# The squared-ReLU MLP of a conformer layer: all first products, then all second products, with the squares kept in DRAM between them

## The chip, the cores and the metric

The kernel runs on one core of a Trainium2 chip. A core has five engines that run their own instruction queues in order: PE (TensorE, matrix products, with a separate row PEld for its weight loads), DVE (VectorE), ACT (ScalarE), POOL (GpSimd) and SP (SyncE, which here only issues DMAs). The metric is the device time of one execution in microseconds (us).

## The reference

One layer on 512 tokens of width 2048: a conformer convolution block, then the MLP, then a last norm. The change touches only the MLP.

```python
h = rmsnorm(x, norm1_g[0]);  x = x + conformer_conv(h, ...)
x = x + sq_relu_mlp(rmsnorm(x, norm2_g[0]), mlp_w1[0], mlp_w2[0])
return rmsnorm(x, final_g)

def sq_relu_mlp(h, w1, w2):
    return jnp.square(jax.nn.relu(h @ w1)) @ w2     # w1: 2048 x 8192, w2: 8192 x 2048
```

## The kernel before

All values are float32, and every product is made of three matmuls of a high part (the value rounded to the matmul type `fp32r`, made by a cast on ACT) and a low part (value minus high part, made by a subtraction): `mm3` at L265 to L270. So each weight chunk that PE uses needs, ahead of it, a DMA, a cast and a subtraction.

**First product.** The width 8192 is cut into 64 tiles f of 128 columns. A tile takes 2 chunks of w1 (128x1024 each) and 48 matmuls of 512 columns. A chunk's low part is made by DVE or POOL (`Plain`, L113). The result is scaled and clipped (L792, DVE) and squared (L793, ACT).

**Second product.** It is made by a seven-product scheme (Winograd's form of Strassen's). Two neighbouring tiles f make a pair; its squares are four 128x256 blocks ("four"), from which three further block sums ("sums") are formed, and the seven blocks are split into high (`ah`) and low (`al`) parts, 128x1792 each (L797, L798). Four pairs make a group; there are 8 groups. On the weight side a group has two halves q, and a half has 14 factors: seven products P1 to P7, each for the inner halves 0 and 1. I write P5.1 for product P5 of inner half 1, and `Factor.make` (L138) builds it: three of the seven are a loaded block as it is (P1, P2, P3), and four are a difference, written in place over a block by POOL (P5 L149, P6 L152, P7 L155, P4 L158). So P5's subtraction may start only once P1's low part has been made from the same block, P6's only after P5's, and so on. Then comes the cast (ACT, L159), two copies of the high part into PSUM (ACT, L162, the tile `ax`) and two subtractions on DVE that read one input from PSUM (L163). A factor takes PE 12 matmuls. The order of the factors in a half is P1.0, P5.0, P2.0, P1.1, P5.1, P2.1, P6.0, P6.1, P3.0, P3.1, P7.0, P7.1, P4.0, P4.1; of P1.1, P5.1 and P2.1 the first six matmuls of each come first, then the other six of each. Finished sums are added from PSUM into the residual on DVE (L834).

**The order before.** Group by group: 8 tiles of the first product, their blocks, then both halves of the second product of the group. The last group has only four tiles in the seven-product form; its other four tiles go through a plain second product with 16 chunks of `w2b`.

**What sets the order of the instructions.** The program is written in the order of the mathematics, and a list scheduler, with its own model of the times, fixes for each engine an order that the engine then follows strictly. A chunk or factor is prepared four ahead of its use (`Stream.AHEAD`), in four buffers `wh` and `wl`: the cast of a factor has to wait until PE is done with the factor four before it.

Of the kernel before, what the change touches and what calls it, by code (L numbers as in the profile page):

```python
# [12 lines left out]
F32 = mybir.dt.float32  # L13
# [5 lines left out]
P = 128  # L19
T = 512  # L20
# [9 lines left out]
POOL_TAPS = 6  # L30

# [29 lines left out]
LEFT = {"P1": 0, "P7": 1, "P4": 2, "P2": 3, "P5": 4, "P6": 5, "P3": 6}  # L61
# [4 lines left out]
OPENS = ("P1", "P5", "P2")  # L66

# [8 lines left out]
def trunk(ctx: ExitStack, tc: tile.TileContext, xT, vec, fg, w_in, w_out, w1, w2s, w2b, out):  # L76
# [10 lines left out]
    front = ExitStack()  # L87
    early = front.enter_context(tc.tile_pool(name="early", bufs=1))
# [41 lines left out]
    class Factor:  # L130
# [7 lines left out]
        def make(self, hi, lo):  # L138
# [20 lines left out]
            nc.scalar.copy(out=hi, in_=s)  # L159
            for sl in (slice(0, 512), slice(512, 1024)):  # L160
                st = bank("ax")
                nc.scalar.copy(out=st, in_=hi[:, sl].bitcast(F32))  # L162
                nc.vector.tensor_tensor(out=lo[:, sl], in0=s[:, sl], in1=st, op=sub)  # L163
# [26 lines left out]
    for q in range(4):  # L190
        items += [Plain(w_out[q, c], nc.gpsimd) for c in range(0 if q else 4, 8)]
    for g in range(NG):
        items += [Plain(w1[g * GROUP + f, c], nc.gpsimd if c else nc.vector) for f in range(GROUP) for c in range(2)]
        if g < NG - 1:
            for q in range(2):
                sums = Sums(w2s[g, q])
                items += [Factor(sums, *x) for x in ORDER]
        else:
            for q in range(2):
                sums = Sums(w2s[g, q])  # L200
                items += [Factor(sums, x, 0) for x, hs in ORDER if hs == 0]
# [55 lines left out]
    def split_scaled(src, g, name):  # L257

        hi = big.tile([P, T], F32R, tag="hh", name=f"{name}h")
        lo = big.tile([P, T], F32R, tag="hl", name=f"{name}l")  # L260
# [331 lines left out]
    class Norm:  # L592


        def __init__(self, k, halves, lo_eng):
            if len(vs) == k:
                vs.append((big.tile([P, T], F32R, tag="hh", name="vh"), big.tile([P, T], F32R, tag="hl", name="vl")))
# [155 lines left out]

    acc = []
    row2 = None
    for g in range(NG):
        last = g == NG - 1
        a = []
        for f in range(GROUP):
            ps = bank()  # L760
            for c in range(2):
                wh, wl = chunk()
                for i in range(8):
                    k = 8 * c + i
                    sl = slice(i * P, (i + 1) * P)
                    mm3(ps, (wh[:, sl], wl[:, sl]), h2[k], k == 0, k == NT - 1)
            if row2 is None:
                st = bank("ax")
                col_sums(st, acc1)
                ms = tmp.tile([P, NTOK], F32, tag="st", name="ms")  # L770
                nc.vector.tensor_scalar(out=ms, in0=st[:, :NTOK], scalar1=1.0 / D, scalar2=None, op0=ALU.mult)
                r2 = spread(inv_sqrt(ms, eps_rms, RMS_EPS, NTOK))
                row2 = shift
                nc.scalar.copy(out=row2, in_=r2)

                for b in range(NTOK):
                    for n in range(4):
                        x2 = big.tile([P, 512], F32, tag="da", name=f"x2_{b}_{n}")
                        pt = bank("ax")
                        for i in range(4):  # L780
                            nc.tensor.transpose(out=pt[:, i * P : (i + 1) * P], in_=xt[4 * n + i][:, b * P : (b + 1) * P], identity=ident)
                        nc.scalar.copy(out=x2, in_=pt)
                        acc.append(x2)
                front.close()
                mlp[0] = ctx.enter_context(tc.tile_pool(name="mlp", bufs=4, reuse_waits="tile"))
            if f % 2 == 0:
                hi = mlp[0].tile([P, 7 * HT], F32R, tag="ah", name="ah")
                lo = mlp[0].tile([P, 7 * HT], F32R, tag="al", name="al")
                four = mlp[0].tile([P, 4 * HT], F32, tag="rb", name="four", bufs=5)
                a.append((hi, lo))  # L790
            here = four[:, f % 2 * T :][:, :T]
            nc.vector.scalar_tensor_tensor(out=here, in0=ps, scalar=0.0, in1=row2, op0=ALU.max, op1=ALU.mult)  # L792
            nc.scalar.activation(out=here, in_=here, func=AF.Square)  # L793

            def split(x, at):
                sl = slice(at * HT, at * HT + x.shape[-1])
                nc.scalar.copy(out=hi[:, sl], in_=x)  # L797
                nc.vector.tensor_tensor(out=lo[:, sl], in0=x, in1=hi[:, sl].bitcast(F32), op=ALU.subtract)  # L798

            a21, a11, a22, a12 = (four[:, i * HT : (i + 1) * HT] for i in range(4))  # L800
            if last and f >= GROUP // 2:
                split(here, f % 2 * 2)
            elif f % 2 == 0:
                sums = mlp[0].tile([P, 4 * HT], F32, tag="rb", name="sums", bufs=5)
# [4 lines left out]
            else:  # L809
# [3 lines left out]
                nc.vector.tensor_tensor(out=s4, in0=a12, in1=s2, op=ALU.subtract)  # L813
                split(sums[:, HT:], 4)

        def seven(q):

            banks = {}

# [134 lines left out]
```

## Time and profile before

| | us |
|---|---|
| median of 3 runs | 1949.85 (1948.09 to 1950.24) |
| the profiled execution: its time | 1946.68 |
| the profiled execution: its span | 1944.8 |
| PE busy | 1889.1 (97%) |
| DVE, ACT, POOL busy | 1251.7, 970.3, 911.2 |

The span is the time from the first to the last instruction. The first product of the MLP begins at 580.71 us. In a row of the timeline stand the start, the duration, the engine, the line, the operation, what it writes and reads, the shape, and in brackets how long the engine had been idle and what released it. Back-to-back matmuls overlap, so a matmul of 0.39 us starts every 0.227 us. In the table by stretches each engine has its busy time, and PEclk is the granted share of TensorE's clock.

### The profile page before, as it was taken

The numbers are of one execution on the slowest core, as the hardware profiler recorded it, in microseconds if no ns is written. First come the engines' busy times: TensorE is split into PE (matmuls) and PEld (weight loads), VectorE is DVE, ScalarE is ACT, GpSimd is POOL, SyncE is SP. The second block draws the span as 40 slices with busy tenths as digits, with TensorE's granted clock in tenths as the row PEclk, the third lists the DMA queues.
The fourth block names the chain that finished last, engine by engine and source line by source line (L and its number), as shares of the span: only waits on it lengthen the run. The fifth ranks groups of instructions, "written<-read, shape, count | busy, mean of one in ns | idle before, by whom it ended". The sixth has DMA issues, their size and how long they took to land.

```text
span 1944.8 us, 22992 instructions
## 1 busy us (share of the span) xinstructions
PE 1889.1 (97%) x8578; PEld 1559.8 (80%) x8578; DVE 1251.7 (64%) x1752; ACT 970.3 (50%) x1406; POOL 911.2 (47%) x475
## 2 busy tenths in 40 slices
PE   6999999989999999999999999999999999999998
PEld 4888888888888877877887887787788778778876
DVE  8999999981044566476466557645754764664485
ACT  5444444473245465367337536634743663473362
POOL 5799999756542252244234224423522442442343
PEclk9999999999999999999999999999999999999999
DMA  5222333114222223322322332232233223223333
GB/s 209 90 98 87 104 123 120 44 52 177 98 97 76 98 97 109 130 81 82 109 87 98 119 130 98 72 102 98 76 130 120 98 87 112 72 91 126 119 93 103
DMA packets 59728, 199.99 MB, mean 103 GB/s; under 512 B 6624, under 2 KB 7264, under 8 KB 59616
## 3 DMA queue, kind: packets, MB, share of 16 engines
q1 hardware_dynamic: 59184, 197.41, 30.0%
q8 instruction: 67, 1.10, 0.2%
q10 hardware_dynamic: 432, 1.11, 0.2%
q14 instruction: 45, 0.37, 0.1%
HBM read 194.31 MB, written 4.19 MB: 102 GB/s over the span
## 4 chain that ended last, share of the span: by engine, by line
PE 71%; DVE 9%; issue 8%; POOL 5%; ACT 4%; DMA 3%; SPq 0%; POOLq 0%; DVEq 0%; ACTq 0%
PE mm L269 21%; PE mm L270 20%; PE mm L268 20%; PE mm L639 8%; DMA b<-in_w2s 2%; POOL b L149 2%; ACT wh L159 2%; DVE wl L163 2%; DVE ax L344 1%; ACT ax L162 1%; POOL b L155 1%; POOL b L158 1%; POOL b L152 1%; DVE x L834 1%; DVE sums L813 1%
## 5 line engine op out<-in xcount | busy, mean ns | idle before, releaser
L113 POOL TENSOR_TENSOR wl<-raw,wh 128x1024 fp32r<-128x1024 f32 x151 | 365.1, 2428 | 620.9 <-ACT wh L112 618.3
L112 ACT CAST wh<-raw 128x1024 fp32r<-128x1024 f32 (+1 forms) x221 | 230.1, 1047 | 452.3 <-PE mm L269 252.4
L269 PE MATMUL mm<-yl,wh 128*128 128x512 f32 x1024 | 398.7, 389 | 0.2 <-DVE yl L262 0.2
L268 PE MATMUL mm<-yh,wh 128*128 128x512 f32 x1024 | 398.7, 389 | 0.0
L270 PE MATMUL mm<-yh,wl 128*128 128x512 f32 x1024 | 398.6, 389 | 0.0
L163 DVE TENSOR_TENSOR wl<-b,ax 128x512 fp32r<-128x512 f32 x420 | 270.2, 681 | 132.1 <-ACT ax L162 95.0
L269 PE MATMUL mm<-wl,ah 128*128 128x512 f32 x840 | 330.1, 393 | 20.4 <-DVE wl L163 20.4
L268 PE MATMUL mm<-wh,ah 128*128 128x512 f32 x840 | 327.0, 391 | 2.3 <-DVE x L834 1.5
L270 PE MATMUL mm<-wh,al 128*128 128x512 f32 x840 | 327.0, 389 | 0.0
L159 ACT CAST wh<-b 128x1024 fp32r<-128x1024 f32 x210 | 217.7, 1050 | 161.8 <-POOL b L149 77.9
L162 ACT COPY ax<-wh 128x512 f32<-128x512 f32 x420 | 234.1, 584 | 13.2 <-DVE wl L163 10.5
L269 PEld LDWEIGHTS mm<-yl,wh 128*128 128x128 f32 x1024 | 192.2, 188 | 40.2 <-DVE yl L262 0.6
L270 PEld LDWEIGHTS mm<-yh,wl 128*128 128x128 f32 x1024 | 192.2, 188 | 40.0
L268 PEld LDWEIGHTS mm<-yh,wh 128*128 128x128 f32 x1024 | 192.2, 188 | 39.7
L344 DVE SCALAR_TENSOR_TENSOR ax<-u,v,ax 128x512 f32<-128x512 f32 x327 | 218.0, 749 | 0.0
L268 PE MATMUL mm<-xh,wh 128*128 128x512 f32 (+1 forms) x544 | 206.9, 380 | 5.9 <-ACT wh L112 5.4
L269 PE MATMUL mm<-xl,wh 128*128 128x512 f32 (+1 forms) x544 | 207.4, 381 | 2.5 <-DVE xl L262 2.4
L270 PE MATMUL mm<-xh,wl 128*128 128x512 f32 (+1 forms) x544 | 206.6, 380 | 3.0 <-DVE wl L113 3.0
L269 PEld LDWEIGHTS mm<-wl,ah 128*128 128x128 f32 x840 | 157.6, 188 | 63.8 <-DVE wl L163 32.3
L268 PEld LDWEIGHTS mm<-wh,ah 128*128 128x128 f32 x840 | 157.6, 188 | 38.3 <-DVE x L834 2.5
L270 PEld LDWEIGHTS mm<-wh,al 128*128 128x128 f32 x840 | 157.7, 188 | 32.0
L149 POOL TENSOR_TENSOR b<-b,b 128x1024 f32<-128x1024 f32 x30 | 74.6, 2486 | 213.6 <-DVE wl L163 213.6
(171 smaller groups left out, 2479.8 us busy)
## 6 DMA issues: line engine op xcount, KB each, us to landing
raw<-in_w SPq DMA_DIRECT2D x128, 512.0 KB, 3.3
b<-in_w2s SPq DMA_DIRECT2D x120, 512.0 KB, 3.6
raw<-in_w_in SPq DMA_DIRECT2D x63, 512.0 KB, 3.3
raw<-in_w_out SPq DMA_DIRECT2D x32, 512.0 KB, 3.3
xt<-in_xT SPq DMA_DIRECT2D x16, 256.0 KB, 5.9
xr<-in_xT SPq DMA_DIRECT2D x16, 256.0 KB, 4.6
raw<-in_w2b SPq DMA_DIRECT2D x16, 256.0 KB, 2.8
out<-x SPq DMA_DIRECT2D x15, 256.0 KB, 2.9
```

What stands on the lines that cost most here:

```text
L112: nc.scalar.copy(out=hi[:, sl], in_=raw[:, sl])
L113: (nc.vector if sl.stop == cut else self.eng).tensor_tensor(out=lo[:, sl], in0=raw[:, sl], in1=hi[:, sl].bitcast(F32), op=ALU.subtract)
L149: nc.gpsimd.tensor_tensor(out=s, in0=b12, in1=b11, op=sub)
L152: nc.gpsimd.tensor_tensor(out=s, in0=b22, in1=b11, op=sub)
L159: nc.scalar.copy(out=hi, in_=s)
L162: nc.scalar.copy(out=st, in_=hi[:, sl].bitcast(F32))
L163: nc.vector.tensor_tensor(out=lo[:, sl], in0=s[:, sl], in1=st, op=sub)
L268: nc.tensor.matmul(out=ps, lhsT=wh, rhs=xh, start=first, stop=False, **how)
L269: nc.tensor.matmul(out=ps, lhsT=wh, rhs=xl, start=False, stop=False, **how)
L270: nc.tensor.matmul(out=ps, lhsT=wl, rhs=xh, start=False, stop=last, **how)
L344: nc.vector.scalar_tensor_tensor(out=o, in0=a, scalar=w, in1=c, op0=ALU.mult, op1=ALU.add)
L639: nc.tensor.matmul(out=ps[n][:, sl], lhsT=a[:, wsl], rhs=x[:, sl], start=first and a is wh and x is hi, stop=last and x is lo)
```

## The change

The first product is now made for all 64 tiles in one go. Of each pair the four blocks and the three sums are written to DRAM (`spill`, 128x1792, by two DMAs on ACT's queue), the sums being made by POOL instead of DVE. Then the second product runs through all 8 groups without a first product between them. `fetch` reads a pair back (SP's queue, two buffers `seven`), `prepare` casts it on ACT in two pieces of 768 and 1024 columns and makes the low parts on DVE. Seven slots hold prepared pairs; slots 3 to 6 lie in the memory of the first product's input `h2`. In the second product, P2's low part is made by POOL straight from the block and its cast (`LO_POOL`), with no copies into PSUM and nothing on DVE. Memory pools are opened from two ends of SBUF. The number of matmuls and their operands' sizes do not change.

```diff
+LO_POOL = ("P2",)
+SLOTS = 7
+PREP = ((0, 3), (0, 9), (1, 2), (1, 12))
+FETCH = ((0, 0), (0, 4), (0, 10), (1, 3))
...
             nc.scalar.copy(out=hi, in_=s)
+            if self.product in LO_POOL:
+                nc.gpsimd.tensor_tensor(out=lo, in0=s, in1=hi.bitcast(F32), op=sub)
+                return
             for sl in (slice(0, 512), slice(512, 1024)):
...
+    for f in range(FF // P):
+        items += [Plain(w1[f, c], nc.gpsimd if c else nc.vector) for c in range(2)]
     for g in range(NG):
-        items += [Plain(w1[g * GROUP + f, c], nc.gpsimd if c else nc.vector) for f in range(GROUP) for c in range(2)]
...
+    def fetch(n):
+        raws[n] = mlp[0].tile([P, 7 * HT], F32, tag="seven", name="seven", bufs=2)
+        width = 7 * HT if n < LASTS else 4 * HT
+        nc.sync.dma_start(out=raws[n][:, :width], in_=spill[n][:, :width])
+
+    def prepare(n):
+
+        seven = raws.pop(n)
+        i = n % SLOTS
+        hi = slots[i].tile([P, 7 * HT], F32R, tag=f"ah{i}", name="ah", bufs=1)
+        lo = slots[i].tile([P, 7 * HT], F32R, tag=f"al{i}", name="al", bufs=1)
+        for sl in (slice(0, 3 * HT), slice(3 * HT, 7 * HT)):
+            nc.scalar.copy(out=hi[:, sl], in_=seven[:, sl])
+            nc.vector.tensor_tensor(out=lo[:, sl], in0=seven[:, sl], in1=hi[:, sl].bitcast(F32), op=ALU.subtract)
+        pairs[n] = (hi, lo)
...
+        if n >= LASTS:
+            nc.scalar.dma_start(out=spill[n][:, f % 2 * T :][:, :T], in_=here)
+        elif f % 2:
             a21, a11, a22, a12 = (four[:, i * HT : (i + 1) * HT] for i in range(4))
...
+            nc.scalar.dma_start(out=spill[n][:, : 3 * HT], in_=four[:, HT:])
+            nc.gpsimd.tensor_tensor(out=s3, in0=a11, in1=a21, op=ALU.subtract)
+            nc.gpsimd.tensor_tensor(out=s1, in0=a21, in1=a22, op=ALU.add)
+            nc.gpsimd.tensor_tensor(out=s2, in0=s1, in1=a11, op=ALU.subtract)
+            nc.gpsimd.tensor_tensor(out=s4, in0=a12, in1=s2, op=ALU.subtract)
+            nc.scalar.dma_start(out=spill[n][:, 3 * HT :], in_=sums)
...
+            for p in range(4 if g < NG - 2 else 2 if g == NG - 2 else 0):
+                if (q, step) == FETCH[p]:
+                    fetch(4 * g + 4 + p)
+                if (q, step) == PREP[p]:
+                    prepare(4 * g + 4 + p)
```

The scheduler's order moves at three places that matter below. All rows are of group 3 (the fourth), and groups 1 to 5 read alike in the change.

**ACT, first half of a group.** Before: `wh_9352`, `wh_9400`, `wh_9435` and `wh_9479` are P5.0, P2.0, P1.1 and P5.1; `four` and `ah` belong to the group's last blocks.

```order
L159 CAST wh_9352<-b11_9241 128x1024
L793 ACTIVATE four_9388<-four_9388 128x512
L162 COPY ax_9356<-wh_9352 128x512
L162 COPY ax_9359<-wh_9352 128x512
L797 CAST ah_9386<-four_9388 128x256
L797 CAST ah_9386<-sums_9391 128x256
L159 CAST wh_9400<-b21_9315 128x1024
L162 COPY ax_9403<-wh_9400 128x512
L162 COPY ax_9406<-wh_9400 128x512
L159 CAST wh_9435<-b11_9350 128x1024
```

The change: `wh_11524`, `wh_11550`, `wh_11574`, `wh_11599` and `wh_11627` are P5.0, P2.0, P1.1, P5.1 and P2.1; `ah` are pairs of the later blocks, cast from `seven`.

```order
L172 CAST wh_11524<-b11_11449 128x1024
L178 COPY ax_11528<-wh_11524 128x512
L178 COPY ax_11531<-wh_11524 128x512
L786 CAST ah_11566<-seven_11347 128x768
L172 CAST wh_11550<-b21_11499 128x1024
L786 CAST ah_11566<-seven_11347 128x1024
L786 CAST ah_11685<-seven_11623 128x768
L172 CAST wh_11574<-b11_11522 128x1024
L786 CAST ah_11685<-seven_11623 128x1024
L178 COPY ax_11577<-wh_11574 128x512
L178 COPY ax_11580<-wh_11574 128x512
L172 CAST wh_11599<-b11_11522 128x1024
```

Between P5.0's and P1.1's copies there now stand the four casts of two whole pairs.

**DVE, the same place in the change.** `wl_11525`, `wl_11575` and `wl_11600` are the low parts of P5.0, P1.1 and P5.1, `al` those of the pairs, `x2` the residual.

```order
L179 TENSOR_TENSOR wl_11525<-b11_11449,ax_11531 128x512
L787 TENSOR_TENSOR al_11567<-seven_11347,ah_11566 128x768
L866 TENSOR_TENSOR x2_0_2_5152<-x2_0_2_5152,mm_11267 128x512
L787 TENSOR_TENSOR al_11567<-seven_11347,ah_11566 128x1024
L866 TENSOR_TENSOR x2_1_2_5180<-x2_1_2_5180,mm_11268 128x512
L787 TENSOR_TENSOR al_11686<-seven_11623,ah_11685 128x768
L179 TENSOR_TENSOR wl_11575<-b11_11522,ax_11577 128x512
L179 TENSOR_TENSOR wl_11575<-b11_11522,ax_11580 128x512
L787 TENSOR_TENSOR al_11686<-seven_11623,ah_11685 128x1024
L179 TENSOR_TENSOR wl_11600<-b11_11522,ax_11603 128x512
```

The low parts of two pairs stand ahead of P1.1's and P5.1's; they read both inputs from SBUF.

**POOL and DVE, second half of a group.** POOL in the change: P5.0, P7.0, P6.0, P2.0's low part, P5.1, P7.1, P2.1's low part, P6.1. Before, the two rows with `wl` were not there.

```order
L162 TENSOR_TENSOR b11_11793<-b12_11817,b11_11793 128x1024
L168 TENSOR_TENSOR b12_11817<-b22_11943,b12_11817 128x1024
L165 TENSOR_TENSOR b11_11793<-b22_11943,b11_11793 128x1024
L174 TENSOR_TENSOR wl_11903<-b21_11849,wh_11902 128x1024
L162 TENSOR_TENSOR b11_11874<-b12_11900,b11_11874 128x1024
L168 TENSOR_TENSOR b12_11900<-b22_11969,b12_11900 128x1024
L174 TENSOR_TENSOR wl_11972<-b21_11918,wh_11971 128x1024
L165 TENSOR_TENSOR b11_11874<-b22_11969,b11_11874 128x1024
```

DVE in the change: an addition to the residual, of P7 of the half before, stands between the two pieces of P1.0's low part (`wl_11852`); before, both pieces came first.

```order
L179 TENSOR_TENSOR wl_11820<-b11_11522,ax_11826 128x512
L179 TENSOR_TENSOR wl_11852<-b11_11793,ax_11854 128x512
L866 TENSOR_TENSOR x2_0_1_5145<-x2_0_1_5145,mm_11609 128x512
L179 TENSOR_TENSOR wl_11852<-b11_11793,ax_11857 128x512
L866 TENSOR_TENSOR x2_1_1_5173<-x2_1_1_5173,mm_11610 128x512
```

Up to the first tiles of the MLP, the instructions stand in the same order on all engines.

234 lines of the change are left out of this document (121 added, 113 removed).

## The prediction

> **What bounds the kernel now.** PE is busy for 97% of the span, so a gain can only come from PE's waits. I first read the table by stretches, for eight first-product tiles and for the second product of a group (group 3) apart.
>
> ```profile
> core 0: us, PE busy (x) PEld busy (x) DVE busy (x) ACT busy (x) POOL busy (x), PEclk, DMA share, GB/s
> 1094.66:1181.25 86.59, 86.59 (x384) 71.70 (x382) 43.26 (x48) 30.97 (x44) 24.08 (x10) 1.00 0.31 105
> 1181.25:1262.15 80.90, 77.97 (x340) 63.05 (x338) 57.01 (x85) 57.00 (x81) 34.07 (x14) 1.00 0.28 96
> ```
>
> The count of weight loads gives the matmuls that start in a stretch. The first product needs 86.59 / 382 = 0.2267 us for one and never idles. At that pace 338 matmuls take 76.62 us; the second product takes 80.90, so 4.28 us per group are lost, 30.0 in the seven full groups. That is the most this change can win, give or take the last group. The list of PE's waits and PE's own rows then say where.
>
> ```profile
> PE mm L269 <- DVE wl L163: 20.4, 28, 1.1
> ...
> 1191.79 0.50 PE L269 MATMUL mm<-wl,ah 128*128 128x512 f32 x1 [0.64 <-DVE wl L163]
> 1194.74 0.50 PE L269 MATMUL mm<-wl,ah 128*128 128x512 f32 x1 [1.07 <-DVE wl L163]
> 1221.63 0.39 PE L268 MATMUL mm<-wh,ah 128*128 128x512 f32 x1
> 1232.50 0.50 PE L269 MATMUL mm<-wl,ah 128*128 128x512 f32 x1 [0.96 <-DVE wl L163]
> 1234.42 0.50 PE L269 MATMUL mm<-wl,ah 128*128 128x512 f32 x1 [0.27 <-DVE wl L163]
> ```
>
> 28 waits are four per group: the low parts of P5.1 and P2.1 in either half. Their brackets sum to 2.94 us; 4.28 - 2.94 over four waits says that a wait costs its bracket and 0.34 more. So the first half loses 2.4 us and the second 1.9. The row at 1221.63 opens the second half; I call such a moment T. PE wants P5.1's low part after 36 + 6 + 1 matmuls, at T + 9.75, and gets it at T + 10.87.
>
> What makes P5.1 late is a chain through three engines, read from the timeline of the second half, where no block work disturbs it.
>
> ```profile
> 1213.67 1.05 ACT L159 CAST wh<-b 128x1024 fp32r<-128x1024 f32 x1 [0.37 <-PE mm L270]
> 1215.38 1.28 DVE L163 TENSOR_TENSOR wl<-b,ax 128x512 fp32r<-128x512 f32 x2 [1.22 <-ACT ax L162]
> 1216.74 2.40 POOL L149 TENSOR_TENSOR b<-b,b 128x1024 f32<-128x1024 f32 x1 [13.65 <-DVE wl L163]
> 1219.22 2.41 POOL L155 TENSOR_TENSOR b<-b,b 128x1024 f32<-128x1024 f32 x1
> 1219.17 1.05 ACT L159 CAST wh<-b 128x1024 fp32r<-128x1024 f32 x1 [3.31 <-POOL b L149]
> 1220.95 1.28 DVE L163 TENSOR_TENSOR wl<-b,ax 128x512 fp32r<-128x512 f32 x2 [3.09 <-ACT ax L162]
> 1221.31 1.05 ACT L159 CAST wh<-b 128x1024 fp32r<-128x1024 f32 x1
> 1222.32 2.41 POOL L152 TENSOR_TENSOR b<-b,b 128x1024 f32<-128x1024 f32 x1 [0.69 <-DVE wl L163]
> 1225.41 1.28 DVE L163 TENSOR_TENSOR wl<-b,ax 128x512 fp32r<-128x512 f32 x2
> 1226.77 2.38 POOL L149 TENSOR_TENSOR b<-b,b 128x1024 f32<-128x1024 f32 x1 [2.04 <-DVE wl L163]
> ```
>
> P1.0's cast waits for its buffer (T - 7.96); its low part ends at T - 4.97; POOL makes P5.0 (T - 4.89), P7.0, P6.0; DVE ends P1.1's low part at T + 5.06 and POOL makes P5.1 from T + 5.14 to 7.52. Cast, copies and low part then take 3.35 us until PE goes on at 1232.50. POOL idles 2.04 us ahead of P5.1: the chain passes through ACT and DVE there, which is where the change puts new work.
>
> **First product: no change in time.** It stays PE's, at 0.2267 us a matmul. DVE loses the sums and splits; POOL gains four 128x256 operations a pair, which I estimate at half of this row each, 0.67 us:
>
> ```profile
> L895 POOL TENSOR_TENSOR x<-x,fgt 128x512 f32<-128x512 f32 x12 | 16.0, 1336 | 21.8 <-ACT sq L893 21.8
> L113 POOL TENSOR_TENSOR wl<-raw,wh 128x1024 fp32r<-128x1024 f32 x151 | 365.1, 2428 | 620.9 <-ACT wh L112 618.3 <-PE mm L269 2.4
> ```
>
> New is that ACT's second spill DMA waits for POOL. Behind it on ACT stand the casts of the next chunks. The worst wait is POOL's chunk plus four sums, 2.43 + 2.68 = 5.1 us, then two casts (2.1) and a low part on POOL (2.4): 9.6. The lookahead is three chunks of 24 matmuls, 16.3 us, which covers it. The spill and fetch add 2 x 0.9 MB per pair, against a DMA share near 0.3; a fetch of 896 KB, by this row scaled, needs some 6.3 us and is issued more than a quarter of a group ahead.
>
> ```profile
> b<-in_w2s SPq DMA_DIRECT2D x120, 512.0 KB, 3.6
> ```
>
> ```profile
> L834 DVE TENSOR_TENSOR x<-x,mm 128x512 f32<-128x512 f32 x224 | 148.1, 682 | 8.4 <-PE mm L270 8.0
> ```
>
> **Second product, second half.** Here three things change. P2's low parts leave ACT and DVE for POOL, 2.4 us each; that removes the wait for P2.1 (0.27 + 0.34) unless POOL is late. But POOL now has P2.0 ahead of P5.1. And P7's addition stands between the halves of P1.0's low part: it waits until PE has finished P7, 24 matmuls ahead of T, and takes 0.68, so it runs from about T - 5.2 to T - 4.5 and P1.0's second piece (0.6) ends at T - 3.9. POOL's P5.0 starts at T - 3.84, 1.05 later. From there on POOL is full: P7.0 until 1.04, P6.0 from 1.5 to 3.9, P2.0 to 6.4 (PE wants it 25 matmuls after T, at 5.67: 0.75 lost), P5.1 from 6.46 to 8.86. PE gets it at 8.86 + 3.35 = 12.2, wanted at 9.75 + 0.85: 1.6 lost. With restarts about 2.8 us in groups 1 to 5. In groups 0 and 6 that addition is not in between: 1.8.
>
> **Second product, first half.** In groups 1 to 5 the order puts into this half the casts and low parts of all four pairs, two of them ahead of P1.1's and P5.1's steps. In group 6, two. Prices:
>
> ```profile
> L797 ACT CAST ah<-sums 128x768 fp32r<-128x768 f32 x30 | 25.0, 834 | 95.3 <-DVE sums L813 95.3
> L113 DVE TENSOR_TENSOR wl<-raw,wh 128x1024 fp32r<-128x1024 f32 x68 | 86.5, 1272 | 123.2 <-ACT wh L112 123.2
> L798 DVE TENSOR_TENSOR al<-sums,ah 128x768 fp32r<-128x768 f32 x30 | 37.3, 1244 | 27.0 <-ACT ah L797 27.0
> ```
>
> On ACT the casts (0.83 and 1.05) stand behind P5.0's copies, which end at T - 0.32 (the cast at 1221.31): pair A to T + 2.5 with P2.0's cast between, B's first piece to 3.3, P1.1's cast to 4.2, B's second piece to 5.2, P1.1's copies to 6.3, low part 7.0. POOL's P5.1 runs from 7.1 to 9.5 and PE has it at 12.8: 3.2 us with the restart, against 2.4 before for both waits. This is the lower bound of the half.
>
> The upper one comes from a conflict that the timeline shows: a DVE subtraction that reads both inputs from SBUF doesn't run while POOL does.
>
> ```profile
> 1160.64 2.40 POOL L113 TENSOR_TENSOR wl<-raw,wh 128x1024 fp32r<-128x1024 f32 x1 [8.49 <-ACT wh L112]
> 1161.12 2.20 DVE L810 TENSOR_TENSOR sums<-four 128x256 f32<-128x256 f32 x1 [0.74 <-ACT four L793]
> ...
> 1182.84 0.42 DVE L810 TENSOR_TENSOR sums<-four 128x256 f32<-128x256 f32 x1 [0.70 <-ACT four L793]
> 1184.99 2.78 POOL L149 TENSOR_TENSOR b<-b,b 128x1024 f32<-128x1024 f32 x1 [7.47 <-DVE wl L163]
> 1185.43 2.62 DVE L813 TENSOR_TENSOR sums<-four,sums 128x256 f32<-128x256 f32 x1
> ```
>
> The same 128x256 operation takes 0.42 us alone and 2.20 beside POOL, where it ends with POOL's. The low parts of factors read one input from PSUM and are spared; the pairs' (L787) are not. With 0.9 and 1.25 us for the two pieces: A's first piece 0.6 to 1.5, POOL's P6.0 only then, to 3.9; A's second piece until 5.1, P2.0's low part to 7.3 (wanted at 5.67: 1.6 lost); B's first piece waits for that, to 8.2; P1.1's low part to 9.4; P5.1 on POOL to 11.9, or to 13.1 if B's second piece goes first; PE goes on at 15.3 or 16.5, wanted at 9.75 + 1.6: 4.0 or 5.2. With restarts the half loses 5.9 to 7.1; I take 6.4, the lower middle, since POOL too can lose the turn (2.78 us at 1184.99).
>
> Group 0's first half is another case: pair 3's slot lies in the memory of `h2`, so its cast waits for PE's last first-product matmul, and ACT's queue with it: between 3.2 and 6.4, I take 3.7 because no other pair stands ahead of P1.1 there; its second half 1.9. The last group has no pair to prepare: as before.
>
> **The sum of waits.** Group 0: 5.6. Groups 1 to 5: 5 x (6.4 + 2.8) = 46.0. Group 6: 6.4 + 1.8 = 8.2. Together 59.8, less the 30.0 of before: +29.8.
>
> **The clock.** A wait of 4 us may also cost TensorE its clock.
>
> ```profile
> 415.66 1.07 PE L639 MATMUL mm<-vl,wh 128*128 128x256 f32 x4 [2.85 <-DVE vl L617]
> ...
> 413.00:416.00 3.00, 0.34 (x2) 0.34 (x3) 2.94 (x4) 0.61 (x2) 1.65 (x1) 0.98 0.00 0
> 416.00:419.30 3.30, 3.30 (x18) 3.28 (x17) 2.75 (x8) 2.42 (x6) 0.73 (x1) 0.50 0.02 5
> ```
>
> After an idle time of 2.85 us PE ran 3.3 us at half clock: 1.65 us lost. After waits near 1 us it kept 1.00 (the second stretch above). There are six first halves with a wait of 4 to 5 us; all of them would cost 6 x 1.65 = 9.9, none 0. I take half, +5. The Trainium skill, "TensorE: Matmul & The Clock Gate", Part 1 ("What's actually happening"), says that the gate closes after an idle window of about 3.4 us whose phase is free-running. By that an idle time of 4 to 5 us holds a whole window in 15 to 45% of cases, an estimate of +1.5 to +4.5 us; the row above, where 2.85 us sufficed, speaks for a shorter one.
>
> The profiled execution was 1946.68 us, 3.2 below the median of the runs; the differences are added to that median: 1949.85 + 29.8 + 5 = 1984.7, rounded to 1984.
>
> **Rivals.**
> *The conflict doesn't count (0.20).* DVE's and POOL's turns fall beside each other. Then first halves lose 3.2: 5.6 + 5 x (3.2 + 2.8) + (3.2 + 1.8) = 40.6, so +10.6, clock kept: 1960. For it: in the order alternate DVE rows read PSUM. Against: POOL is full from T - 3.8 to T + 8, so a pair's low part finds it running.
> *Faster (0.15).* If a wait for P5.1 as long as the shortest before (0.64 + 0.34, or 1.2 with P2.0 slightly late) is all that stays in each half, 14 x 1.2 = 16.8 against 30.0 give 1937. It needs the casts of the pairs to run ahead of the order's other rows, that is P5.0's copies to end some 2 us ahead of T - 0.32. For it: ACT idled 3.3 us ahead of P5.0's cast and DVE as much. Against: that idle time ends with POOL's P5.0, which isn't earlier in the change.
> *No change that can be measured (0.07).* Without the conflict, and with the addition free to pass in the second halves: 5.6 + 6 x 5.0 = 35.6, so 5.6 above, within reach of a small error.
> *First product slower (0.06).* If the fetches, casts and spill DMAs hold ACT for 13 us rather than 5 at each pair, casts and low part make it 17.5 against a lookahead of 16.3: 1.2 us at 30 pairs, +36 on top, 2020. Against: nothing found that holds ACT so long.
>
> **How the numbers follow.** The forecast has 0.52, from 1972 (5.9 per half, no clock loss) to 1998 (7.1, all six clock losses, and 0.7 at P3.0 in each). A measurement here can't tell less than 0.2%, 3.9 us, from no change. Faster 0.15, same 0.07, slower 0.52 + 0.20 + 0.06 = 0.78. The range runs from 1941, which leaves out the better part of the faster case, to 1998.
>
> **What would show it.** Right: the first product at 86.6 us per eight tiles; no wait for P2.1; L787 rows of over 2 us beside POOL; first halves with a wait of 3 to 5 us at P5.1's L179 low part and one near 1.5 at P2.0's L174, after which PEclk drops to near 0.5 in some; second halves at 2 to 3 us. Wrong: halves without a wait beyond 1 us, L787 at 0.9 to 1.3 us, or PE waiting on L113 in the first product. What would undo the number is P1.1's low part ending before T + 6.

## The result, and the profile after

The changed kernel takes 1998.12 us (median of 4 runs, 1997.83 to 2000.39); the kernel before took 1950.03 us beside it. The ratio is 1.0251, with a 95% interval of 1.0234 to 1.0269: 48 us slower. The forecast was slower by 34 us, with a range that ended at 1998, so the direction was right and the time lies just outside.

The profiled execution took 1997.83 us, with a span of 1996.0; before, the span was 1944.8. So 51.2 us have to be found in the trace. The table by stretches shows eight tiles' worth of the first product, and then the first and the second half of group 4.

```profile
core 0: us, PE busy (x) PEld busy (x) DVE busy (x) ACT busy (x) POOL busy (x), PEclk, DMA share, GB/s
1100.00:1187.00 87.00, 87.00 (x386) 72.03 (x385) 15.30 (x17) 21.32 (x24) 30.61 (x24) 1.00 0.40 139
1633.10:1680.71 47.61, 41.92 (x169) 33.02 (x168) 37.79 (x46) 32.41 (x45) 25.38 (x10) 0.93 0.47 166
1680.71:1721.53 40.82, 38.93 (x170) 31.30 (x168) 24.58 (x40) 27.93 (x41) 24.79 (x11) 1.00 0.31 103
```

The first product is as before: 87.0 us for 385 matmuls is 0.226 us each, PE never idle. A half of the second product has 168 matmuls, which take 168 x 0.2267 = 38.08 us without waits. Below, what a half takes beyond this is called its loss. The first half loses 47.61 - 38.08 = 9.53 us, and PEclk is 0.93 in it; the second loses 2.74. Measured in this way, from the first matmul of each half to that of the next, the 14 halves of the full groups lose 77.1 us against 29.6 before (the prediction's 30.0 is seven times group 3's 4.28). The last group with its plain product takes 88.85 us from its first to its last matmul, against 84.87. Together: 77.1 - 29.6 + 4.0 = 51.5; the first product begins 0.3 us earlier in the profiled execution of the changed kernel (580.45 against 580.71), which leaves the 51.2.

The list of PE's waits has three lines where before there was one of 20.4 us:

```profile
PE mm L281 <- DVE wl L179: 24.9, 23, 1.7
PE mm L280 <- ACT wh L172: 14.3, 7, 2.3
PE mm L281 <- POOL wl L174: 11.8, 12, 1.3
```

In 6 of the 7 first halves PE now waits even for the high part of P5.1 (the second line), 2.3 us each, and then for its low part. PE's rows of group 4's first half, which opens at 1633.10, show the three waits in their order: P2.0's low part from POOL, P5.1's cast, P5.1's low part.

```profile
1640.25 0.50 PE L281 MATMUL mm<-wl,ah 128*128 128x512 f32 x1 [1.32 <-POOL wl L174]
1646.70 0.73 PE L280 MATMUL mm<-wh,ah 128*128 128x512 f32 x2 [2.30 <-ACT wh L172]
1648.91 0.80 PE L281 MATMUL mm<-wl,ah 128*128 128x512 f32 x1 [1.48 <-DVE wl L179]
```

The prediction had P2.0's low part at T + 7.3 and P5.1's at T + 15.3 or 16.5; they come at T + 7.15 and T + 15.8. The engines behind it, from the timeline of the same place, DVE first and then POOL:

```profile
1633.64 0.96 DVE L787 TENSOR_TENSOR al<-seven,ah 128x768 fp32r<-128x768 f32 x1
1634.52 0.68 DVE L866 TENSOR_TENSOR x<-x,mm 128x512 f32<-128x512 f32 x1
1635.54 2.42 DVE L787 TENSOR_TENSOR al<-seven,ah 128x1024 fp32r<-128x1024 f32 x1 [0.34 <-ACT ah L786]
1637.88 0.68 DVE L866 TENSOR_TENSOR x<-x,mm 128x512 f32<-128x512 f32 x1
1638.48 2.53 DVE L787 TENSOR_TENSOR al<-seven,ah 128x768 fp32r<-128x768 f32 x1
1640.93 1.27 DVE L179 TENSOR_TENSOR wl<-b,ax 128x512 fp32r<-128x512 f32 x2
1642.13 1.21 DVE L787 TENSOR_TENSOR al<-seven,ah 128x1024 fp32r<-128x1024 f32 x1
```

```profile
1633.79 3.09 POOL L165 TENSOR_TENSOR b<-b,b 128x1024 f32<-128x1024 f32 x1 [0.69 <-DVE wl L179]
1636.84 3.35 POOL L174 TENSOR_TENSOR wl<-b,wh 128x1024 fp32r<-128x1024 f32 x1
1642.28 3.29 POOL L162 TENSOR_TENSOR b<-b,b 128x1024 f32<-128x1024 f32 x1 [2.09 <-DVE wl L179]
```

A pair's 768 columns take DVE 0.96 us while POOL waits, and 2.53 us where they come second. POOL's operations of 2.4 us take 3.1 to 3.35. P1.1's low part, which stood at T + 3.8 in the second halves before, is made at T + 7.8 (1640.93), and POOL's P5.1 begins at T + 9.2 instead of T + 5.1.

What follows the three waits is a slower clock, PEclk 0.50 from 1647.59 to 1654.41:

```profile
1644.18:1647.59 3.41, 0.95 (x3) 0.30 (x2) 0.00 (x0) 1.99 (x3) 3.33 (x2) 1.00 0.83 269
1647.59:1651.00 3.41, 2.09 (x5) 1.70 (x6) 1.94 (x3) 3.41 (x7) 3.41 (x3) 0.50 0.00 0
1651.00:1654.41 3.41, 3.41 (x9) 2.64 (x9) 3.41 (x3) 2.03 (x3) 1.68 (x1) 0.50 0.00 0
```

PE waits for the first 1.3 us of this (until 1648.91). In the 5.5 us that are left it starts 13 matmuls, where 24 fit at 0.2267 us each.

### The profile page after: what moved, and what is told of

The parts are those of the page before. It is cut to its first block, busy times and chain, and to the rows that moved or that the text cites. A ratio compares the mean times of both kernels' runs of the same rounds, so it can differ in the third digit from the quotient of the medians.

```text
span 1996.0 us, 23068 instructions
## 1 busy us (share of the span) xinstructions
PE 1908.2 (96%) x8578; PEld 1567.2 (79%) x8578; DVE 1082.8 (54%) x1512; ACT 923.3 (46%) x1286; POOL 1084.5 (54%) x625
## 4 chain that ended last, share of the span: by engine, by line
PE 58%; DVE 14%; issue 12%; POOL 10%; DMA 3%; ACT 1%; SPq 0%; POOLq 0%; DVEq 0%; ACTq 0%
PE mm L281 17%; PE mm L282 16%; PE mm L280 16%; PE mm L651 8%; DVE ax L356 4%; POOL b L162 4%; POOL b L168 3%; DMA b<-in_w2s 3%; DVE wl L179 2%; DVE x L866 2%; POOL wl L174 2%; POOL b L171 1%; DVE al L787 1%; POOL b L165 1%; DVE xl L274 1%
## 5 line engine op out<-in xcount | busy, mean ns | idle before, releaser
L281 PE MATMUL mm<-wl,ah 128*128 128x512 f32 x840 | 339.3, 404 | 36.7 <-DVE wl L179 24.9
L280 PE MATMUL mm<-wh,ah 128*128 128x512 f32 x840 | 331.2, 397 | 16.2 <-ACT wh L172 14.3
L282 PE MATMUL mm<-wh,al 128*128 128x512 f32 x840 | 332.9, 397 | 0.0
L179 DVE TENSOR_TENSOR wl<-b,ax 128x512 fp32r<-128x512 f32 x360 | 231.5, 681 | 169.0 <-ACT ax L178 92.6
L126 DVE TENSOR_TENSOR wl<-raw,wh 128x1024 fp32r<-128x1024 f32 (+1 forms) x70 | 89.5, 1279 | 353.8 <-ACT wh L125 353.8
L178 ACT COPY ax<-wh 128x512 f32<-128x512 f32 x360 | 200.6, 585 | 17.7 <-DVE wl L179 15.1
```

Source lines behind the costliest of these rows:

```text
L126: (nc.vector if sl.stop == cut else self.eng).tensor_tensor(out=lo[:, sl], in0=raw[:, sl], in1=hi[:, sl].bitcast(F32), op=ALU.subtract)
L280: nc.tensor.matmul(out=ps, lhsT=wh, rhs=xh, start=first, stop=False, **how)
L281: nc.tensor.matmul(out=ps, lhsT=wh, rhs=xl, start=False, stop=False, **how)
L282: nc.tensor.matmul(out=ps, lhsT=wl, rhs=xh, start=False, stop=last, **how)
```

## The experiments

I had one theory and three rivals. The theory: pairs are prepared where P5.1's chain passes, and the pairs' subtractions on DVE and POOL's operations hold each other up. The rivals: it is the casts on ACT alone; it is P2's low parts on POOL; it is the traffic to and from DRAM. The first kernels take single pieces out of the change.

**The preparation left out.**

```diff
-left = tuple(y[:, o : o + P] for y in pairs[4 * g + 2 * hs + i])
+left = tuple(y[:, o : o + P] for y in pairs[2 * hs + i])
-for p in range(4 if g < NG - 2 else 2 if g == NG - 2 else 0):
+for p in range(0):
```

> The changed kernel, but the second product of every group reads the four pairs that were prepared first: from group 1 on no pair is fetched, cast or subtracted (its output is not the reference's). First theory (the preparation of the pairs in the first halves is the cause): first halves fall from 9.3 us lost to 2 to 3, like the second halves; no half clock in them, no wait at P4.0; time 1950 to 1957. Rival (P2's low parts on POOL, or the spill's traffic, are the cause): first halves still lose over 6 us, time above 1975.

Measured: 1947.79 us, ratio 0.9995 (0.9983 to 1.0006). Every half from the second on loses 1.72 us. Group 3's first half:

```profile
1526.19:1565.99 39.80, 38.58 (x169) 31.36 (x168) 24.07 (x40) 27.04 (x39) 23.80 (x11) 1.00 0.33 106
```

The whole loss of the change hangs on the preparation, or on the fetches that go with it. The first halves came out better than I expected (1.72, not 2 to 3): without pairs in the order, the addition between the pieces of P1.0's low part is gone as well. The halves then lose 23.5 us, 6.1 less than before, but the last group takes 90.9 us, 6.0 more than before, and the time is the same.

**The casts kept, the subtractions left out.**

```diff
-lo = slots[i].tile([P, 7 * HT], F32R, tag=f"al{i}", name="al", bufs=1)
+lo = slots[i].tile([P, 7 * HT], F32R, tag=f"al{i}", name="al", bufs=1) if n < 4 else pairs[n % 4][1]
     nc.scalar.copy(out=hi[:, sl], in_=seven[:, sl])
-    nc.vector.tensor_tensor(out=lo[:, sl], in0=seven[:, sl], in1=hi[:, sl].bitcast(F32), op=ALU.subtract)
+    if n < 4:
+        nc.vector.tensor_tensor(out=lo[:, sl], in0=seven[:, sl], in1=hi[:, sl].bitcast(F32), op=ALU.subtract)
```

> The changed kernel, with the pairs' casts on ACT kept and the pairs' subtractions on DVE (L787) left out from group 1 on; the second product reads the low parts of the first four pairs instead (its output is not the reference's). First theory (DVE's subtractions with two SBUF inputs meet POOL, and that adds to the casts): no wait at P2.0 in first halves, P5.1's wait 3 to 3.5 us, clock kept, so 3 to 4 us lost in each and a time of 1960 to 1968. Rival (the casts on ACT alone): first halves stay above 7 us, time above 1983.

**The subtractions kept, the casts left out.**

```diff
-hi = slots[i].tile([P, 7 * HT], F32R, tag=f"ah{i}", name="ah", bufs=1)
+hi = slots[i].tile([P, 7 * HT], F32R, tag=f"ah{i}", name="ah", bufs=1) if n < 4 else pairs[n % 4][0]
-    nc.scalar.copy(out=hi[:, sl], in_=seven[:, sl])
+    if n < 4:
+        nc.scalar.copy(out=hi[:, sl], in_=seven[:, sl])
```

> The changed kernel, with the pairs' subtractions on DVE kept and their casts on ACT left out from group 1 on; the subtractions read the casts of the first four pairs (its output is not the reference's). First theory: the subtractions still wait for POOL and POOL for them: P2.0's wait of about 1.5 us stays, P5.1's falls by 1 to 2 us, first halves lose 5 to 8 us, time 1972 to 1990. Rival (the casts on ACT alone): first halves fall to 2 to 3 us, time 1950 to 1958.

Measured: 1960.84 us with the casts alone (ratio 1.0056, 1.0034 to 1.0079), 1995.44 us with the subtractions alone (1.0245, 1.0212 to 1.0278). With the casts alone there is no wait at P2.0, and POOL's operations take their 2.4 us: the first halves of groups 1 to 6 lose 3.0 where the clock holds and 4.05 where it doesn't. With the subtractions alone they lose 8.4 to 9.7, as much as with both. POOL's rows of group 3's first half in that kernel, and then PE's:

```profile
1545.90 3.38 POOL L165 TENSOR_TENSOR b<-b,b 128x1024 f32<-128x1024 f32 x1
1549.23 3.08 POOL L174 TENSOR_TENSOR wl<-b,wh 128x1024 fp32r<-128x1024 f32 x1
1554.68 3.02 POOL L162 TENSOR_TENSOR b<-b,b 128x1024 f32<-128x1024 f32 x1 [2.36 <-DVE wl L179]
```

```profile
1552.37 0.50 PE L281 MATMUL mm<-wl,ah 128*128 128x512 f32 x1 [1.07 <-POOL wl L174]
1558.82 0.73 PE L280 MATMUL mm<-wh,ah 128*128 128x512 f32 x2 [2.29 <-ACT wh L172]
```

So the two are not parts of a sum: 3.7 us with one, 9.0 with the other, 9.3 with both. The subtractions on DVE are enough for the whole loss. My expectation that P5.1's wait would fall by 1 to 2 us without the casts was wrong: the scheduler, with ACT free, put still more subtractions (three pairs and a half) ahead of P5.1's low part.

**The subtractions read PSUM.** This asks whether it is the second SBUF input or the mere amount of work.

```diff
+if n >= 4:
+    for sl in (slice(0, 512), slice(512, 768), slice(768, 1280), slice(1280, 1792)):
+        st = bank("ax")[:, : sl.stop - sl.start]
+        nc.scalar.copy(out=st, in_=hi[:, sl].bitcast(F32))
+        nc.vector.tensor_tensor(out=lo[:, sl], in0=seven[:, sl], in1=st, op=ALU.subtract)
```

> The changed kernel, but from group 1 on the pairs' subtractions read their second input from PSUM, to which ACT copies the first four pairs' casts (2.05 us a pair, in place of 1.88 us of casts; its output is not the reference's). ACT's and DVE's work is as large as in the change; only the second SBUF input of DVE's instruction is gone. First theory (it is the meeting with POOL that costs): no instruction of the pairs on DVE takes over 0.75 us, POOL's take 2.4, no wait at P2.0, first halves lose 2 to 4.5 us, time 1950 to 1968. Rival (the amount of work on DVE and ACT costs, whatever it reads): first halves above 7 us, time above 1982.

Measured: 1987.49 us (1.0203, 1.0183 to 1.0223), so the time was not what the theory said. The table by stretches for group 3, first half and second half, and the groups of L789:

```profile
1541.38:1582.91 41.53, 39.41 (x170) 31.15 (x168) 29.83 (x51) 30.63 (x47) 19.68 (x10) 1.00 0.45 150
1582.91:1626.89 43.98, 41.38 (x170) 32.15 (x168) 26.60 (x43) 30.72 (x45) 27.90 (x12) 0.96 0.39 134
```

```profile
L789 DVE TENSOR_TENSOR al<-seven,ax 128x512 fp32r<-128x512 f32 x78 | 51.1, 682 | 1.9 <-ACT ax L788 1.0
L174 POOL TENSOR_TENSOR wl<-b,wh 128x1024 fp32r<-128x1024 f32 x30 | 72.9, 2430 | 0.6 <-ACT wh L172 0.6
```

The mechanism is as expected: 682 ns for each piece, none beside POOL longer than alone, POOL at 2.43 us instead of 2.61 in the change, first halves at 3.4 us. But the second halves lose 4.9 to 5.9, where the change lost 2.7: in the new order only one pair stands ahead of P1.1 in the first half, and the work on the others goes on later, ahead of the next half. So the meeting with POOL is shown. What it costs by itself this kernel can't say: two pairs stood ahead of P1.1 in the change, so the fall of the first halves from 9.3 to 3.4 us can't be put down to PSUM alone, and the work that was moved is paid for in the second halves.

**P2's low parts back on ACT and DVE.**

```diff
-LO_POOL = ("P2",)
+LO_POOL = ()
```

> The changed kernel with P2's low parts back on ACT and DVE, as before the change. First theory: P2.0's wait goes and POOL has 4.8 us less in each half, but the copies and subtractions of P2 stand in the queues of ACT and DVE again, and the pairs stay: first halves lose 6 to 10 us, second halves 1.9, time 1980 to 1995. Rival (P2 on POOL is the main harm): first halves below 4 us, time below 1968.

Measured: 1977.65 us (1.0154, 1.0103 to 1.0205), 20 us better than the change and a little better than I expected. First halves lose 5.5 us on average, second halves 2.6. So P2 on POOL is a good part of the harm, though not the main one by the bounds set. To see it by itself, the kernel before was given this part alone:

```diff
+            if self.product == "P2":
+                nc.gpsimd.tensor_tensor(out=lo, in0=s, in1=hi.bitcast(F32), op=sub)
+                return
```

> The kernel before with one part of the change alone: P2's low parts are made by POOL. First theory (a DVE subtraction with two SBUF inputs and a POOL operation hold each other up): second halves improve a little, from 1.9 to 1.7 us lost, since P2.1's wait goes and P5.1's stays; in the first halves the blocks' work on DVE meets the added POOL work and the half loses 2 to 4 us instead of 2.4; time 1946 to 1960. Rival (POOL's new work harms only through its own queue): first halves lose no more than second halves, time 1944 to 1947.

Measured: 1984.03 us (1.019, 1.0171 to 1.0209): 36 us slower, far outside of what either theory said. PE's two waits in group 3's first half, and POOL's rows there:

```profile
1204.61 0.50 PE L272 MATMUL mm<-wl,ah 128*128 128x512 f32 x1 [0.64 <-DVE wl L166]
1209.96 0.50 PE L272 MATMUL mm<-wl,ah 128*128 128x512 f32 x1 [3.68 <-POOL wl L161]
```

```profile
1205.23 2.38 POOL L152 TENSOR_TENSOR b<-b,b 128x1024 f32<-128x1024 f32 x1 [2.09 <-DVE wl L166]
1207.56 2.35 POOL L161 TENSOR_TENSOR wl<-b,wh 128x1024 fp32r<-128x1024 f32 x1
```

It is POOL's queue. P2.1's low part (L161) stands behind P6.1 (L152). P6.1 begins at 1205.23; P2.1's cast on ACT runs from 1204.33 to 1205.38, so P2.1 misses its turn by 0.15 us and waits 2.2 us for P6.1. PE wanted it at 1206.1, and the operation itself takes 2.35 us on POOL; so 2.2 of the 3.68 us are the order, the rest is POOL's own time after a late cast. Half clock follows. Neither row is longer than 2.4 us, so the meeting of DVE and POOL plays no part in this wait. In the change's own order P2.1 stands ahead of P6.1, so this is not the harm that the diff before this one removed: there P2.0 takes 2.4 us of POOL, 3.35 beside a pair's subtraction, ahead of P5.1.

**A fifth buffer.** P5.1's chain begins with a cast that waits for a buffer, four factors back. The change leaves 8 KB free per partition in the second product, enough for one more `wh` and `wl`.

```diff
+            k = i - FIRST
+            fifth = 0 <= k < 28 * (NG - 1) and k % 5 == 4
+            pool = late_pool[0] if fifth else wts
-            hi = wts.tile([P, 1024], F32R, tag="wh", name="wh")
+            hi = pool.tile([P, 1024], F32R, tag="wh", name="wh", bufs=1 if fifth else 4)
```

> The changed kernel with a fifth buffer for the factors (wh and wl) in the second product, in 8 KB per partition that the change leaves free there, and preparation five ahead; pairs as in the change. Every cast of a factor may start one factor, 2.7 us, earlier. First theory (P5.1's chain is late by 1.4 us in second halves and by some 4 in first halves, by its buffer and by what stands ahead of it): second halves lose 0 to 0.5 us, first halves 2 to 5, time 1940 to 1963. Rival (DVE and POOL have simply too much to do in first halves, so an earlier start is used up): first halves stay above 7 us, time above 1968.

Measured: 1997.05 us (1.0254, 1.0236 to 1.0272), no change. The rival's numbers came true: the earlier start is used up (7.7 to 10.6 us lost in the first halves of groups 1 to 6). PE's waits for P5.1's cast are gone, but those for its low part remain, up to 2.7 us, and another is now the longest, for an addition to the residual:

```profile
PE mm L285 <- DVE x L872: 26.4, 13, 2.9
```

```profile
1569.53 1.33 DVE L792 TENSOR_TENSOR al<-seven,ah 128x768 fp32r<-128x768 f32 x1 [2.92 <-ACT ah L791]
1570.78 1.27 DVE L179 TENSOR_TENSOR wl<-b,ax 128x512 fp32r<-128x512 f32 x2
1571.97 1.87 DVE L872 TENSOR_TENSOR x<-x,mm 128x512 f32<-128x512 f32 x3
```

P6.0 needs the banks that this addition empties; it stands in DVE's queue behind a pair's subtraction, which waits 2.92 us for its cast. Here DVE is idle and can't go on, so what uses up the start in this place is the order of its queue, and not, as the rival had it, too much work.

**The pairs are split in the first product.** There DVE is busy for 15.3 of 87.0 us and ACT for 21.3. High and low parts are both written to DRAM and read straight into the slots.

```diff
+hi = slots[k].tile([P, 7 * HT], F32R, tag=f"ah{k}", name="ah", bufs=1)
+lo = slots[k].tile([P, 7 * HT], F32R, tag=f"al{k}", name="al", bufs=1)
+for src, sl in ((four[:, HT:], slice(0, 3 * HT)), (sums, slice(3 * HT, 7 * HT))):
+    nc.scalar.copy(out=hi[:, sl], in_=src)
+    nc.vector.tensor_tensor(out=lo[:, sl], in0=src, in1=hi[:, sl].bitcast(F32), op=ALU.subtract)
+nc.sync.dma_start(out=spill_h[n], in_=hi.bitcast(F32))
+nc.sync.dma_start(out=spill_l[n], in_=lo.bitcast(F32))
...
+nc.sync.dma_start(out=hi.bitcast(F32), in_=spill_h[n])
+nc.sync.dma_start(out=lo.bitcast(F32), in_=spill_l[n])
```

> The changed kernel, but the pairs are cast and split in the first product, where ACT and DVE have time, and both parts are written to DRAM and read back straight into the pairs' slots: no work of ACT and DVE on pairs in the second product, twice the spill traffic (1.8 MB per pair each way). First theory (the place of the preparation is the harm, not the traffic): all halves lose 1.7 to 1.8 us as where the preparation was left out, time 1945 to 1952. Rival (the transfers delay the weights): waits for DMA appear, time above 1956.

> The kernel that spills both parts, with the fifth buffer for the factors as well. First theory: with the pairs' work away and every factor's chain 2.7 us earlier, P5.1's low part is there before PE wants it; the halves lose 0 to 0.5 us each instead of 1.7, time 1920 to 1932. Rival (P5.1 waits for POOL's queue, not for its buffer): halves still lose over 1.2 us, time above 1940.

Measured: 1952.82 us with four buffers (1.0024, 1.0014 to 1.0033), 1947.57 us with five (0.9998, 0.9988 to 1.0008). With four, 12 of the 14 halves lose 1.7 us, as with the preparation left out. The two others lose 4.4 and 4.3, and their rows name no transfer: in group 0 PE waits 2.49 us for P2.1's low part in POOL's queue, and in group 6 the chain of P5.1 is late behind subtractions that the change has there for the last group:

```profile
1774.00 2.83 DVE L906 TENSOR_TENSOR al<-seven,ah 128x512 fp32r<-128x512 f32 x1 [0.92 <-ACT ah L905]
1777.95 3.47 DVE L906 TENSOR_TENSOR al<-seven,ah 128x512 fp32r<-128x512 f32 x2
```

That settles the rival of the traffic: twice as much of it delays nothing that PE waits for in the halves. With five, PE's wait for P5.1 is gone and another has come in its place, neither 0 to 0.5 us nor the rival's:

```profile
PE mm L286 <- POOL wl L174: 16.3, 12, 3.7
```

It is the same place in POOL's queue as above: the scheduler put P2.1's low part behind P6.1 again, and PE gets it 1.2 us late in nine of the 14 halves, 1.6 to 3.8 in three others; one of these also loses its clock, 6.8 us in all. In group 3's first half P6.1 begins at 1536.43 and lasts 2.4 us; P2.1's cast ends at about the same moment (it is the first of two casts that take 2.00 us from 1535.43), so it has missed its turn again. So P2 was taken off POOL here too (`LO_POOL = ()`), with five buffers and with four:

> The kernel that spills both parts and has the fifth buffer, with P2's low parts back on ACT and DVE. First theory (once the pairs are gone and the buffers are five, what is left is P2.1's low part at the end of POOL's queue, 1.2 us and its restart in nearly every half): that wait goes, the halves lose 0 to 0.6 us, time 1918 to 1932. Rival (ACT and DVE need P2's work away to keep pace): halves lose 1.5 us or more at P5.1 or P2.1, time above 1943.

> Both parts spilled, P2's low parts on ACT and DVE, four buffers: the last kernel without its fifth buffer. First theory (the wait for P5.1 is set by the buffer of P1.1 and P5.1): every half loses 2.4 to 2.6 us, as second halves did with P2 back (1.8 at P5.1, 0.4 at P2.1 and restarts); time 1953 to 1962. Rival (the fifth buffer adds little once P2 is back): halves lose under 1 us, time below 1935.

Measured: 1926.34 us with five buffers (0.9887, 0.9871 to 0.9904) and 1947.69 us with four (1.0000, 0.9990 to 1.0010). With four, 12 of the 14 halves lose 1.8 us at P5.1 and P2.1, less than the 2.4 to 2.6 I had taken from a kernel with pairs in it. With five they lose 0.2 to 0.6 in all but one; group 3's first half has no wait worth the name:

```profile
1521.39:1559.65 38.26, 38.26 (x169) 31.40 (x168) 26.41 (x42) 29.15 (x43) 19.41 (x9) 1.00 0.70 278
```

This kernel is faster than the change and, by 1.1%, than the kernel before. Its sum: the halves lose 5.6 us instead of 29.6, the last group takes 87.3 instead of 84.9, so 21.6 less. From the start of the first product on, the profiled execution is 21.4 us shorter than before, and the medians differ by 21.3.

**The change with the fifth buffer and with P2 off POOL, its preparation unmoved.**

> The changed kernel with the fifth buffer and P2's low parts back on ACT and DVE; the pairs are prepared in the second product as in the change. First theory (the pairs' subtractions meet POOL in first halves, whatever else is mended): second halves lose 0.2 to 0.6 us, first halves 2 to 6, time 1936 to 1962. Rival (with P2 off POOL and earlier casts the pairs are covered): first halves lose under 1 us, time below 1932.

Measured: 1963.02 us (1.0084, 1.0066 to 1.0102): first halves 4.8 us, as expected, second halves 1.7, more than the 0.2 to 0.6 expected; the time is 1 us above the range of the first theory. The pairs in the second product cost 37 us against the kernel above even then. Side by side, with the mean loss of a half in groups 1 to 6 (the kernel before took 1947 to 1950 us beside each):

| pairs split | P2's low part | buffers | us | first half | second half |
|---|---|---|---|---|---|
| second product (the change) | POOL | 4 | 1998.1 | 9.3 | 2.7 |
| second product | POOL | 5 | 1997.1 | 9.2 | 2.5 |
| second product | DVE | 4 | 1977.7 | 5.5 | 2.6 |
| second product | DVE | 5 | 1963.0 | 4.8 | 1.7 |
| first product | POOL | 4 | 1952.8 | 2.1 | 1.7 |
| first product | DVE | 4 | 1947.7 | 2.2 | 1.8 |
| first product | POOL | 5 | 1947.6 | 1.4 | 1.7 |
| first product | DVE | 5 | 1926.3 | 0.5 | 0.4 |

With the pairs split in the first product, each repair alone is worth 5 us and both together 26: behind either wait stood the other.

## Why the prediction was right or wrong

**Right: what bounds the kernel, and that no more than 30 us could be won.** The best kernel here won 21 with the halves' losses almost gone.

**Right: the first product doesn't change.** It has no wait, and ACT's spill DMAs delay nothing there.

**Right: the second halves.** 2.8 us were forecast for groups 1 to 5, 2.64 to 2.74 measured, at P2.0 (0.8) and P5.1 (1.4) as worked out. Group 6 was given 1.8 and lost 2.7: its order has P2.0's wait as well.

**Right: the mechanism of the first halves, and their waits.** The steps of the working are the rows of the trace to half a microsecond, the mutual delay of DVE and POOL among them. The waits at P2.0 and P5.1 came to 5.8 us with their restarts, against 6.4 forecast. That it is the subtractions and not the casts was not said so sharply; the prediction's lower bound (casts alone, 3.2) is what the kernel with the casts alone showed (3.0 with the clock kept).

**Wrong: the clock, the step "I take half, +5".** All six first halves of groups 1 to 6 lost the clock, and not each for one stretch of 3.3 us: in groups 1 and 2 the half clock lasts 3.41 us, in groups 3 to 6 it lasts 6.83. So on average each paid 2.5 us for it, not 1.65: what is left of the six losses when the waits are taken off is 14.8 us, from some 1.5 in group 1 to some 3 in groups 5 and 6. That is 9.8 more than taken, and more than the upper bound of 9.9. This is the largest error of the sum. The wait comes in two pieces, 2.30 and 1.48 with two matmuls between, which I had as one. The sentence on the Trainium skill said 15 to 45% of cases, 1.5 to 4.5 us; it was further off than the row.

**Wrong: "the half loses" P2.0 and P5.1 and nothing more.** The working stopped at P5.1. At the end of the first halves of groups 1 to 5 P4.0's low part is late by 0.75 us with 0.11 for the restart, behind the subtractions of the last two pairs on DVE, and P3.0's in groups 1 and 2 by half a microsecond; with 0.6 in group 6 this is 6.2 us in the six halves. In group 4 DVE works without a pause until 1673.92, and 5.1 us of its work after 1659.89 are those subtractions:

```profile
1659.89 3.05 DVE L787 TENSOR_TENSOR al<-seven,ah 128x1024 fp32r<-128x1024 f32 x1
1667.65 2.08 DVE L787 TENSOR_TENSOR al<-seven,ah 128x768 fp32r<-128x768 f32 x2
1675.59 0.50 PE L281 MATMUL mm<-wl,ah 128*128 128x512 f32 x1 [0.59 <-DVE wl L179]
```

In the kernel without the preparation and in the one with the casts alone this wait is not there. The prediction listed P3.0 only in its range, and P4.0 not at all.

**Wrong: "The last group ... as before."** It takes 4.0 us more. In the trace PE waits there 1.5 us for an addition to the residual and 1.7 for a low part, and then runs 7 matmuls at half clock; before, its longest wait in the last group was 1.2.

```profile
1916.97 0.50 PE L280 MATMUL mm<-wh,ah 128*128 128x512 f32 x1 [1.51 <-DVE x L866]
1930.16 0.50 PE L281 MATMUL mm<-wl,ah 128*128 128x512 f32 x1 [1.73 <-DVE wl L179]
```

With P2's low parts back it takes 2.2 us more than before; what makes up that rest was not taken apart.

The sum, for the profiled executions: 34.8 forecast, +9.8 for the clock, +6.2 at P4.0 and P3.0, +4.0 in the last group, -3.5 for P2.0 and P5.1 in first halves, -0.1 for group 0 and the second halves together: 51.2. (The 29.6 in place of 30.0 would add 0.4, the earlier start of the first product takes 0.3 off.) The medians differ by 48.1, since the profiled execution before was 3.4 us below its median of 1950.03, and the one after 0.3 below its own.

**Wrong, without effect: the lower end of the range.** 5.9 us a half and no clock loss give 5.6 + 5 x 8.7 + 7.7 = 56.8 us of waits, 26.8 more than 30.0, so 1976.7 and not 1972. The upper end does follow from its terms, 1998.0, and the measured time lies 0.1 above it; but it holds 9.9 for the clock and 4.2 for P3.0, where 14.8 and 6.2 were found, nothing for the last group's 4.0, and waits of 7.1 us a half, where 5.8 were found. That it came so near is partly luck: what it put too high nearly made up for what it put too low or left out.

**The rivals.** That the conflict doesn't count, on which the rival of no change rests too, is refuted by POOL's rows of 3.09 to 3.35 us and by the kernel with the subtractions alone. "Faster" needed casts that run ahead; it didn't happen in this kernel. A time below its 1937 can be had, but in another way: with the pairs' work moved to the first product, P2 off POOL and a fifth buffer it is 1926. That the first product leaves its pace did not occur.

## What to carry to other kernels

Before work is moved into a stage, follow the chain on which that stage's bottleneck engine waits, engine by engine in queue order, and go on to the end of the stage: the first wait found is not the last. An operation handed to an idle engine is not free if that engine's queue is strict, for it waits behind whatever stands ahead, ready or not. And where two repairs each bring little, try both: here each was worth 5 us and the two 26.

## What the runs showed of the hardware

**The clock falls on a fixed grid, and without a full idle stretch.** In the kernel with the casts alone, the same three waits stand in six first halves (0.91, 0.38 and 0.70 us with their restarts, within 3.2 us); in groups 1 and 2 the clock holds, in groups 3 to 6 it falls. The ends of the half-clock stretches lie on a grid of 3.413 us that goes on through the whole kernel: those of the changed kernel's groups 1 to 4 are 88.7 to 88.8 us apart, 26 steps, while the groups themselves begin 87.9 to 88.0 us apart, and that of group 6 lies 52 steps behind group 4's. Cut on this grid, the stretches of group 1 (two), group 2 (two) and group 3 (with the one after it) of the kernel with the casts alone read, and below them three of the changed kernel's group 2:

```profile
1375.09:1378.50 3.41, 2.66 (x12) 1.68 (x10) 0.00 (x0) 2.98 (x4) 3.33 (x2) 1.00 0.68 209
1378.50:1381.91 3.41, 2.36 (x8) 1.25 (x8) 1.28 (x2) 3.41 (x6) 3.41 (x3) 1.00 0.50 210
1457.00:1460.42 3.42, 2.45 (x9) 1.15 (x7) 0.14 (x1) 2.96 (x5) 3.34 (x3) 1.00 0.68 229
1460.42:1463.83 3.41, 2.56 (x11) 1.75 (x11) 2.03 (x4) 3.41 (x6) 3.41 (x2) 1.00 0.18 74
1538.93:1542.34 3.41, 1.92 (x6) 1.01 (x7) 1.20 (x2) 3.41 (x5) 3.41 (x2) 0.99 0.77 269
1542.34:1545.75 3.41, 3.41 (x10) 2.38 (x9) 1.37 (x3) 2.93 (x5) 3.41 (x3) 0.51 0.00 0
```

```profile
1466.69:1470.10 3.41, 1.83 (x9) 1.17 (x7) 0.77 (x1) 0.38 (x1) 3.33 (x2) 1.00 0.46 120
1470.10:1473.51 3.41, 1.21 (x4) 0.73 (x5) 1.22 (x2) 3.41 (x5) 3.41 (x2) 1.00 0.36 152
1473.51:1476.92 3.41, 3.41 (x10) 2.62 (x9) 2.52 (x2) 3.41 (x6) 3.29 (x2) 0.50 0.00 0
```

In the kernel with the casts alone a stretch with PE busy for 1.92 of its 3.41 us is followed by half clock, and stretches with 2.36 and more are not. In the changed kernel a stretch with 1.83 is not followed by it, and the next one, with 1.21, is. The Trainium skill, "TensorE: Matmul & The Clock Gate", Part 1 ("What's actually happening"), gives a free-running window of 3413 ns, with which the grid agrees; that the window must be idle is not what these rows show. No single bound on PE's busy time as the profile counts it fits both kernels (1.92 fell, 1.83 held); what decides besides the grid stays open.

**A DVE subtraction with two SBUF inputs and a POOL operation hold each other up in both directions.** In group 4's rows above, whichever comes second ends late: DVE 2.53 us instead of 0.96, POOL 3.1 to 3.4 instead of 2.4. With one input in PSUM DVE's pieces of 512 columns take 0.682 us and POOL's low parts 2.43, hardly longer than alone.
